# A second layer's input projections as seven products of halves instead of eight

## The chip, the cores and the metric

One core of a Trainium2 chip. The number is the device time of one execution in microseconds (us). The kernel before was run three times: 1753.05, 1754.44 and 1762.82 us, a median of 1754.44. One further execution was recorded by the profiler; every row below is of that one.

## What is computed

An encoder of two residual layers on 512 tokens of width 2048, in float32. Layer 0 mixes a gated DeltaNet and grouped query attention, and ends in an output projection with a residual. Layer 1, which the change is about, is a gated MLP:

```python
def gmlp_layer(x, norm_g, w_in, ln_g, ln_b, w_s, b_s, w_out):
    h = rms_norm(x, norm_g)
    u, v, gate = jnp.split(h @ w_in, 3, axis=-1)
    u = jax.nn.gelu(u, approximate=False)
    v = layer_norm(jax.nn.gelu(v, approximate=False), ln_g, ln_b)
    vc = v.reshape(bsz, n, C_CHUNK, C_GROUPS, cg)
    s = jnp.einsum('gts,bnsgc->bntgc', w_s, vc) + jnp.transpose(b_s)[None, None, :, :, None]
    z = u * s.reshape(bsz, L, C_WIDTH) * jax.nn.silu(gate)
    return x + z @ w_out
```

`h @ w_in` is 512 x 2048 by 2048 x 6144: one third each for u, v and gate.

## The kernel before

All big products are made by `proj` (L245) in groups of 512 output columns, in this order: layer 0's input groups, O0 to O3 (layer 0's output projection), VV0 to VV3 (v of layer 1), GG0, UU0, GG1, UU1 up to UU3 (gate and u in turn), R0 to R3 (layer 1's output projection). A group is 16 K-blocks of 128 rows of the weights. For one K-block each of the four blocks of 128 tokens takes three matmuls of 128x512 into its own PSUM bank, because every float32 operand is held as a high part (fp32r) and a rest: high by high, high by rest, rest by high (L276 to L278). That is 12 matmuls per K-block, 192 per group.

`load_raw` (L214) brings the weights, two K-blocks in one 512 KB transfer on SyncE's queue, into three buffers `raw`. `split` (L223) makes the high part `whi` by a cast on ScalarE (L231) and the rest `wlo` by a subtraction on VectorE (L232). `proj` calls it for the K-block at hand and the next two, and there are three buffers of each, so a split can begin when the K-block three back has been used. Splits run over the group's end into the next group.

When a group's last K-block is issued, the group is evacuated from its four banks: `evac` of O (L1252, L1255: residual and squares), of VV (L1294, Gelu, then BN_STATS2 at L1299), of GG (L1332, Silu), of UU (L1339, Gelu). All other work is written as generators in three lanes; `sub` (L171), called between the blocks of matmuls, runs as much of them as a rate allows, so an engine's order is that of the calls. `force` drains a lane for a result that is needed at once. The background work of this part: `h1_turn` (h = normalised x, transposed and split), `layer_norm1` (L1305, over v, which stays in SBUF), `spatial` (L1342: for each of 16 groups of 128 columns the product with w_s, times u and gate, and transposes to z), and `z_split` (L1403), whose first two row blocks are made ten K-blocks into UU3. Every engine works its instructions off in order.

## Time and profile before

| | |
|---|---|
| median of three runs | 1754.44 us (1753.05 to 1762.82) |
| span of the profiled execution | 1752.8 us (of its own whole time nothing more is recorded) |
| TensorE busy | 1723.6 us, 98% of the span |
| VectorE, ScalarE, GpSimd busy | 870.7, 718.6, 214.5 us |
| memory read and written | 125 GB/s over the span |

The span runs from the first to the last instruction of the one recorded execution. Busy time counts an engine's computing instructions; matmuls overlap in the array, so TensorE's busy share says that it always had work, not how fast it did it. Chain shares are of the span, along the chain of instructions and waits that ended last.

### The profile page before, as it was taken

How to read it: one execution, taken by the hardware profiler on the slowest of the kernel's cores; microseconds unless marked ns; L12 is line 12 of the kernel's file. 1: busy time of each engine (PE TensorE's matmuls, PEld its weight loads, DVE VectorE, ACT ScalarE, POOL GpSimd, SP SyncE). 2: the span in 40 equal slices, each digit the busy share in tenths (PEclk: the TensorE clock that was granted, in tenths of full speed). 3: DMA queues.
4: the chain of work that ended last, by engine and by line, in shares of the span. 5: the costliest groups of instructions: out<-in, count | busy, mean ns of one | idle time of the engine just before them, and what ended most of it. 6: DMA issues, size and time to landing. Idle time of an engine off the chain costs nothing.

```text
span 1752.8 us, 22461 instructions
## 1 busy us (share of the span) xinstructions
PE 1723.6 (98%) x8285; PEld 1426.1 (81%) x8285; DVE 870.7 (50%) x1544; ACT 718.6 (41%) x1463; POOL 214.5 (12%) x247
## 2 busy tenths in 40 slices
PE   8999998999999999999999999999999999999999
PEld 8888886787888998888788888888888888888887
DVE  4555599642764777876533333337342424235332
ACT  6444443524655555665422332222343433343221
POOL 0110055420200323540100000000000000000000
PEclk9999999979999999999999999999999999999999
DMA  5534642695464556434534443332323233333443
GB/s 191 140 94 123 127 115 81 138 200 146 116 172 122 165 162 193 148 94 157 169 121 137 144 156 97 96 97 89 105 89 96 84 96 90 96 109 100 145 140 109
DMA packets 212797, 221.30 MB, mean 126 GB/s; under 512 B 97857, under 2 KB 124785, under 8 KB 212688
## 3 DMA queue, kind: packets, MB, share of 16 engines
q1 hardware_dynamic: 211104, 215.33, 42.3%
q0 software_dynamic: 1408, 4.40, 1.0%
q8 instruction: 65, 1.06, 0.3%
q14 instruction: 44, 0.36, 0.1%
q10 hardware_dynamic: 176, 0.14, 0.0%
HBM read 186.18 MB, written 33.65 MB: 125 GB/s over the span
## 4 chain that ended last, share of the span: by engine, by line
PE 88%; DVE 5%; ACT 2%; issue 2%; SPq 1%; DMA 1%; POOL 0%; ACTq 0%; DVEq 0%; POOLq 0%
PE acc L277 20%; PE acc L276 20%; PE acc L278 20%; PE acc L272 5%; PE acc L273 5%; PE acc L274 5%; PE su L864 1%; DVE wlo L232 1%; PE mg L755 1%; PE aux L84 1%; DVE cv L437 1%; DMA raw<-in_w_in_dram 1%; PE sc L846 1%; PE po L1095 1%; DVE pr L661 1%
## 5 line engine op out<-in xcount | busy, mean ns | idle before, releaser
L232 DVE TENSOR_TENSOR wlo<-raw,whi 128x512 fp32r<-128x512 f32 (+1 forms) x544 | 387.8, 714 | 733.0 <-ACT whi L231 725.6
L231 ACT CAST whi<-raw 128x512 fp32r<-128x512 f32 (+1 forms) x544 | 330.0, 607 | 721.1 <-PE acc L278 534.5
L276 PE MATMUL acc<-whi,h1h 128*128 128x512 f32 x768 | 304.5, 396 | 0.0
L278 PE MATMUL acc<-whi,h1l 128*128 128x512 f32 x768 | 303.3, 395 | 0.0
L277 PE MATMUL acc<-wlo,h1h 128*128 128x512 f32 x768 | 303.3, 395 | 0.0
L272 PE MATMUL acc<-hTh,whi 128*128 128x512 f32 x512 | 211.9, 414 | 0.9 <-ACT whi L231 0.9
L274 PE MATMUL acc<-hTh,wlo 128*128 128x512 f32 x512 | 204.3, 399 | 7.2 <-DVE wlo L232 7.2
L273 PE MATMUL acc<-hTl,whi 128*128 128x512 f32 x512 | 203.5, 398 | 0.0
L278 PEld LDWEIGHTS acc<-whi,h1l 128*128 128x128 f32 x768 | 144.0, 187 | 35.1
L277 PEld LDWEIGHTS acc<-wlo,h1h 128*128 128x128 f32 x768 | 144.0, 188 | 34.8
L276 PEld LDWEIGHTS acc<-whi,h1h 128*128 128x128 f32 x768 | 144.0, 187 | 34.5
L276 PE MATMUL acc<-whi,hTh 128*128 128x352 f32 (+1 forms) x384 | 161.6, 421 | 1.4 <-ACT whi L231 1.4
L277 PE MATMUL acc<-wlo,hTh 128*128 128x352 f32 (+1 forms) x384 | 139.9, 364 | 3.1 <-DVE wlo L232 3.1
L278 PE MATMUL acc<-whi,hTl 128*128 128x352 f32 (+1 forms) x384 | 139.2, 363 | 0.0
L274 PEld LDWEIGHTS acc<-hTh,wlo 128*128 128x128 f32 x512 | 96.8, 189 | 32.9 <-DVE wlo L232 9.8
L272 PEld LDWEIGHTS acc<-hTh,whi 128*128 128x128 f32 x512 | 97.0, 189 | 19.4 <-ACT whi L231 1.0
L273 PEld LDWEIGHTS acc<-hTl,whi 128*128 128x128 f32 x512 | 97.1, 190 | 18.5
L276 PE MATMUL acc<-whi,zh 128*128 128x512 f32 x224 | 87.2, 389 | 0.0
L277 PE MATMUL acc<-wlo,zh 128*128 128x512 f32 x224 | 86.9, 388 | 0.0
L278 PE MATMUL acc<-whi,zl 128*128 128x512 f32 x224 | 86.9, 388 | 0.0
L277 PEld LDWEIGHTS acc<-wlo,hTh 128*128 128x128 f32 x384 | 74.1, 193 | 10.0 <-DVE wlo L232 4.5
L278 PEld LDWEIGHTS acc<-whi,hTl 128*128 128x128 f32 x384 | 73.4, 191 | 8.6
(315 smaller groups left out, 2489.9 us busy)
## 6 DMA issues: line engine op xcount, KB each, us to landing
raw<-in_w_in_dram SPq DMA_DIRECT2D x184, 512.0 KB, 3.8
raw<-in_w_out_dram SPq DMA_DIRECT2D x64, 512.0 KB, 3.7
raw<-in_w_in_dram SPq DMA_DIRECT2D x24, 352.0 KB, 4.1
...
```

The lines of the kernel that those rows point to most:

```text
L84: nc.tensor.transpose(out=o, in_=i, identity=ident[:k, :k])
L231: nc.scalar.copy(hi[:, :n], raw[:, a, :n])
L232: nc.vector.tensor_sub(lo[:, :n], raw[:, a, :n], hi[:, :n].bitcast(F32))
L272: mm(pt, lhsT=hi[:, s], rhs=ah, start=f, stop=False)
L273: mm(pt, lhsT=hi[:, s], rhs=al, start=False, stop=False)
L274: mm(pt, lhsT=lo[:, s], rhs=ah, start=False, stop=l)
L276: mm(pt, lhsT=ah[:, s], rhs=hi[:, cs], start=f, stop=False)
L277: mm(pt, lhsT=ah[:, s], rhs=lo[:, cs], start=False, stop=False)
L278: mm(pt, lhsT=al[:, s], rhs=hi[:, cs], start=False, stop=l)
L437: nc.vector.scalar_tensor_tensor(v[:, a:b], s[:, a + o:b + o], tp(j), v[:, a:b], ALU.mult, ALU.add)
L661: eng.tensor_tensor(pr, M[:, z, j + 1:, j:j + 1].to_broadcast(sj), W[:, z, j:j + 1, 0:n].to_broadcast(sj), op=ALU.mult)
L755: mm(pt[:, gs], lhsT=bd[:, w, g, :], rhs=src[:, gs], start=True, stop=True)
```

## The change

VV, GG and UU are made by a new function `fast` instead of `proj`. It halves tokens, K and the group's columns: 256 tokens by 256 columns, with each K-slab of 512 rows holding four quarters B11, B12, B21, B22 of the weights. Instead of eight products of quarters it makes seven (one level of Strassen's scheme in Winograd's form), each a sum over four slabs: of B11, B21, B22 and of four differences of quarters, T1 to T4. Each product has its own PSUM bank for the whole group.

- A unit is one product in one slab: 28 units per group, each 12 matmuls of 128x256. A product's first matmul (`opening`) is 128x512, with a half of zeros, and so starts the whole bank. The look-ahead of two units and the three buffers stay; `whi` is now three places in one constant tile.
- `tee` makes T1 to T4 of a slab on GpSimd, 16 subtractions of 128x512 per group (in `ex`); `split` works on quarters and differences, 28 times a group.
- `operands` makes the seven combinations of h that the products take: per pair of K-blocks four sums on GpSimd, three casts and three subtractions. Those of the second half of K follow O3, within VV0. For them O's evacuation keeps a scaled copy `xs` (one more activation per tile).
- `combine` puts the products together: one copy and seven additions per group. A product's turn comes in the unit behind its last one; T4's comes behind the group. Activations follow in place on T1's and T4's turn, two each, and for v the stores and BN_STATS2.
- v goes to DRAM (`v_d`) and comes back in tiles of 128 columns, which `spatial` normalises one by one. z goes to DRAM too, as far as it is ready before R0, and z's first two row blocks are split between UU3 and R0 (`z_firsts`). w_s is loaded on SyncE's queue, the layer norm's gains by each `spatial`. R's residual tiles are loaded later in their group.

```diff
+    FAST = {f"{m}{j}" for m in ("VV", "GG", "UU") for j in range(4)}
+    ORDER = ("B11", "B21", "B22", "T2", "T1", "T3", "T4")
+    units, start_of = [], {}
+    for gi, g in enumerate(groups):
+        start_of[g[0]] = len(units)
+        units += [(gi, k) for k in range(28 if g[0] in FAST else KT)]
     LOOK = 2
...
+        if nm in FAST:
+            src = w[(q // 2) * 512:(q // 2 + 1) * 512, c0:c0 + n].rearrange("(a e p) c -> e p a c", p=P, e=2)[q % 2]
...
+    whi_ = cst("whi", [P, 2 * LOOK + 3, 256], F32R)
+    nc.scalar.activation(whi_[:, 2 * LOOK + 2, :], ones.unsqueeze(1).to_broadcast([P, 2, P]), AF.Copy, scale=0.0)
+    def whi(u):
+        r = 2 * (u % (LOOK + 1))
+        return whi_[:, r:r + 2, :].rearrange("p a c -> p (a c)")
+    def opening(u):
+        r = 2 * (u % (LOOK + 1))
+        return whi_[:, r::2 * LOOK + 2 - r, :][:, 0:2, :]
...
+    def tee(gi, sl, nm):
+        t = ex(int(nm[1]) - 1).rearrange("p (a c) -> p a c", a=2)
+        q = lambda z: quarter(gi, sl, z)
+        a, b = {"T1": (lambda: (q("B12"), q("B11"))), "T2": (lambda: (q("B22"), tees[gi, sl, "T1"])),
+                "T3": (lambda: (q("B22"), q("B12"))), "T4": (lambda: (q("B21"), tees[gi, sl, "T2"]))}[nm]()
+        nc.gpsimd.tensor_tensor(t, a, b, op=ALU.subtract)
+        tees[gi, sl, nm] = t
+    def ahead(u):
+        for d, nm in ((2, "T1"), (1, "T2"), (0, "T3"), (-1, "T4")):
+            if 0 <= u + d < len(units):
+                gi, k = units[u + d]
+                if groups[gi][0] in FAST and k % 7 == (0 if d >= 0 else 1 + d) and (gi, k // 7, nm) not in tees:
+                    tee(gi, k // 7, nm)
+                    if nm in ("T3", "T4"):
+                        gone[0] = gi * 8 + (k // 7) * 2 + (1 if nm == "T3" else 2)
...
-        raw = raws[qi]
-        hi = sb.tile([P, 512], F32R, tag="whi", bufs=LOOK + 1, name=uid("whi"))
+        gi, k = units[u]
+        nm, _, _, n, _ = groups[gi]
+        hi = whi(u)
         lo = sb.tile([P, 512], F32R, tag="wlo", bufs=LOOK + 1, name=uid("wlo"))
-        nc.scalar.copy(hi[:, :n], raw[:, a, :n])
-        nc.vector.tensor_sub(lo[:, :n], raw[:, a, :n], hi[:, :n].bitcast(F32))
-        splits[i] = (hi, lo)
-        if a == 0:
-            load_raw(qi + 2)
+        if nm in FAST:
+            sl, o = k // 7, ORDER[k % 7]
+            src = quarter(gi, sl, o) if o[0] == "B" else tees[gi, sl, o]
+            v = lambda z: z.rearrange("p (a c) -> p a c", a=2)
+        else:
+            qi, a = gi * 8 + k // 2, k % 2
+            src = raws[qi][:, a, :n]
+            v = lambda z: z[:, :n]
+            if a:
+                gone[0] = qi + 1
+        nc.scalar.copy(v(hi), src)
+        nc.vector.tensor_sub(v(lo), src, v(hi).bitcast(F32))
+        splits[u] = (hi, lo)
...
+    def fast(name, ops, evac, late=None, func=None, rate=0.2):
+        u0 = pos[0]
+        gi = units[u0][0]
+        assert groups[gi][0] == name and u0 == start_of[name], name
+        bank = {o: (chain() if z in (4, 5) else aux("prod") if z == 6 else acc()) for z, o in enumerate(ORDER)}
+        todo = []
+        for u in range(u0, u0 + 28):
+            sl, o = (u - u0) // 7, ORDER[(u - u0) % 7]
+            pump()
+            for z in range(LOOK + 1):
+                split(u + z)
+            ahead(u)
+            if late is not None and u == u0 + 21:
+                late()
+            if func is not None and u == u0 + 20:
+                warm(func)
+            hi, lo = splits[u]
+            for kk in range(2):
+                a = ops(sl * 2 + kk)
+                for tb in range(2):
+                    out = bank[o][:, tb * 256:tb * 256 + 256]
+                    ah, al = (a(o, w)[:, tb * P:(tb + 1) * P] for w in range(2))
+                    h, l = (z[:, kk * 256:kk * 256 + 256] for z in (hi, lo))
+                    e = sl == 3 and kk == 1 and tb == 1
+                    if sl == 0 and kk == 0 and tb == 0:
+                        mm(bank[o], lhsT=ah, rhs=opening(u), start=True, stop=False)
+                    else:
+                        mm(out, lhsT=ah, rhs=h, start=False, stop=False)
+                    mm(out, lhsT=ah, rhs=l, start=False, stop=False)
+                    mm(out, lhsT=al, rhs=h, start=False, stop=e)
+                if kk == 0 and todo:
+                    evac(*todo.pop(0))
+                sub(1.0, rate)
+            splits.pop(u)
+            if sl == 3:
+                todo.append((o, bank))
+        for z in todo:
+            evac(*z)
+        pos[0] = u0 + 28
+    def combine(dst):
+        t = {}
+        def f(o, bank):
+            v = lambda z: bank[z].rearrange("p (t c) -> p t c", t=2)
+            tt = lambda a, b, c: nc.vector.tensor_add(a, b, c)
+            if o == "B11":
+                t["1"] = st("pp", [P, 2, 256])
+                nc.scalar.copy(t["1"], v(o))
+            elif o == "B21":
+                tt(dst("C11"), v(o), t["1"])
+            elif o == "T2":
+                t["2"] = st("pp", [P, 2, 256])
+                tt(t["2"], v(o), t["1"])
+                tt(dst("C12"), v("B22"), t["2"])
+            elif o == "T1":
+                tt(dst("C12"), v(o), dst("C12"))
+            elif o == "T3":
+                tt(t["2"], v(o), t["2"])
+                tt(dst("C22"), v("T1"), t["2"])
+            elif o == "T4":
+                tt(dst("C21"), v(o), t["2"])
+        return f
...
             spill(x1_d[t * P:(t + 1) * P, js], z)
+            xs.append(st("xs", [P, 512]))
+            nc.scalar.activation(xs[t], z, AF.Copy, scale=sc1[:, t:t + 1])
             jk = st("jk", [P, 512])
-            nc.scalar.activation(jk, z, AF.Square, accum_out=ss1[:, t, j:j + 1])
+            nc.scalar.activation(jk, xs[t], AF.Square, accum_out=ss1[:, t, j:j + 1])
...
+        g = lambda x, y, z, op: nc.gpsimd.tensor_tensor(x, y, z, op=op)
+        g(s[:, 0], a21, a22, ALU.add)
+        g(s[:, 1], s[:, 0], a11, ALU.subtract)
+        g(s[:, 2], a11, a21, ALU.subtract)
+        g(s[:, 3], a12, s[:, 1], ALU.subtract)
+        for src, z in ((hq[:, :, 0:256], opA[b][:, i]), (a22, opH[0][:, p])):
+            nc.scalar.copy(z[:, 0], src)
+            nc.vector.tensor_sub(z[:, 1], src, z[:, 0].bitcast(F32))
+            yield 0.8
+        yield -3
+        z = opS[p // 2][:, p % 2]
+        nc.scalar.copy(z[:, 0], s)
+        nc.vector.tensor_sub(z[:, 1], s, z[:, 0].bitcast(F32))
+        yield 1.2
...
+        def f(o, bank):
+            gu(o, bank)
+            if o in ("T1", "T4"):
+                for t in ((0, 1) if o == "T1" else (2, 3)):
+                    z = into[t // 2][:, t % 2, :]
+                    front.add(stats(z, t, j))
+                    spill(v_d[j * 4:j * 4 + 4, :, t, :].rearrange("g p c -> p g c"), z.rearrange("p (g c) -> p g c", g=4))
...
+    def fast_gu(into, func):
+        into.extend(m4("gu", [P, 2, 512]) for _ in range(2))
+        dst = lambda c: into[c[1] == "2"][:, :, (c[2] == "2") * 256:(c[2] == "2") * 256 + 256]
+        com = combine(dst)
+        def f(o, bank):
+            com(o, bank)
+            if o in ("T1", "T4"):
+                for t in range(2):
+                    z = into[o == "T4"][:, t, :]
+                    tt = t + 2 * (o == "T4")
+                    nc.scalar.activation(z, z, func, scale=rs1[:, tt:tt + 1])
+        return f
...
-        proj(f"VV{j}", act1, evac_v1(j), func=AF.Gelu if j == 0 else None)
...
+        fast(f"VV{j}", act1, fast_v1(j), func=AF.Gelu if j == 0 else None, rate=0.3)
...
+    def z_firsts():
+        for k in range(2):
+            z_split(k, zld.pop(k))
...
-        proj(f"GG{j}", act1, gate_evac(sgs), func=AF.Silu)
-        proj(f"UU{j}", act1, u_evac(us), func=AF.Gelu, late=(lambda: (z_split(0), z_split(1))) if j == 3 else None)
+        fast(f"GG{j}", act1, fast_gu(sgs, AF.Silu), func=AF.Silu)
+        fast(f"UU{j}", act1, fast_gu(us, AF.Gelu), func=AF.Gelu, late=z_first if j == 3 else None)
         front.add(spatial(j, us, sgs))
-    # ---------------- final projection ----------------
+    z_firsts()
```

The change moves work at the ends of the groups. Three places show it; the numbers behind tile names tell buffers apart.

VectorE where GG0 ends and UU0 begins, before: the subtractions of `split` (`wlo`) of UU0's first four K-blocks, with one row of `layer_norm1`.

```order
L232 TENSOR_TENSOR wlo_10607<-raw_10530,whi_10606 128x512
L1322 TENSOR_TENSOR vt_9446<-vt_9446,lg_10335 128x1024
L232 TENSOR_TENSOR wlo_10626<-raw_10530,whi_10625 128x512
L232 TENSOR_TENSOR wlo_10652<-raw_10571,whi_10651 128x512
L232 TENSOR_TENSOR wlo_10670<-raw_10571,whi_10669 128x512
```

The same place with the change: `acc`, `chain` and `prod` are PSUM banks, `gu` the group's result, `pp` a running sum.

```order
L308 TENSOR_TENSOR wlo_11849<-ex_8882,whi 128x512
L427 TENSOR_TENSOR pp_11858<-acc_11436,pp_11808 128x512
L427 TENSOR_TENSOR gu_11431<-acc_11435,pp_11858 128x2x256
L308 TENSOR_TENSOR wlo_11867<-raw_11700,whi 128x512
L427 TENSOR_TENSOR gu_11431<-chain_11437,gu_11431 128x2x256
L308 TENSOR_TENSOR wlo_11886<-raw_11796,whi 128x512
L427 TENSOR_TENSOR pp_11858<-chain_11438,pp_11858 128x512
L427 TENSOR_TENSOR gu_11432<-chain_11437,pp_11858 128x2x256
L427 TENSOR_TENSOR gu_11432<-prod_11439,pp_11858 128x2x256
L308 TENSOR_TENSOR wlo_11916<-raw_11796,whi 128x512
```

The first row is unit 27, the last of GG0; the three other subtractions are UU0's units 0, 1 and 2. Six additions that were not there lie between them: two for T2, T1's ahead of unit 1, and T3's two and T4's ahead of unit 2.

ScalarE at the same place, before: four activations of GG0's results stand between the casts of UU0's K-blocks 1 and 2, in one piece.

```order
L231 CAST whi_10606<-raw_10530 128x512
L231 CAST whi_10625<-raw_10530 128x512
L1332 ACTIVATE sg_1828_10632<-acc_10316,rs_9140 128x512
L1332 ACTIVATE sg_1828_10632<-acc_10317,rs_9140 128x512
L1332 ACTIVATE sg_1829_10641<-acc_10318,rs_9140 128x512
L1332 ACTIVATE sg_1829_10641<-acc_10319,rs_9140 128x512
L231 CAST whi_10651<-raw_10571 128x512
L231 CAST whi_10669<-raw_10571 128x512
```

And with the change:

```order
L430 COPY pp_11808<-acc_11433 128x512
L307 CAST whi<-ex_8882 128x512 x3
L307 CAST whi<-raw_11700 128x512
L1527 ACTIVATE gu_11431<-gu_11431,rs_8933 128x512 x2
L307 CAST whi<-raw_11796 128x512
L1527 ACTIVATE gu_11432<-gu_11432,rs_8933 128x512 x2
L307 CAST whi<-raw_11796 128x512
L307 CAST whi<-ex_8882 128x512 x4
```

The three casts from `raw` are those of UU0's units 0, 1 and 2. T1's two activations, which take what VectorE's additions leave, now stand ahead of unit 1's cast, and T4's two ahead of unit 2's.

ScalarE where UU3 ends and R0 begins, with the change (`z` and `zl` are z's row blocks, from DRAM):

```order
L307 CAST whi<-raw_14868 128x512
L1527 ACTIVATE gu_14573<-gu_14573,rs_8933 128x512 x2
L307 CAST whi<-raw_14868 128x512
L1527 ACTIVATE gu_14574<-gu_14574,rs_8933 128x512 x2
L1554 CAST z_1974_15101<-zl_14969 128x512
L1554 CAST z_1975_15102<-zl_14971 128x512
L307 CAST whi<-raw_14985 128x512
```

The casts of z's first two row blocks, which R0's first matmuls take, have come from the middle of UU3 to behind T4's activations.

## Rows read from the trace of the kernel before

**Rows 1.** The page: the span, and the shares of the chain that ended last

```profile
span 1752.8 us, 22461 instructions
...
PE 88%; DVE 5%; ACT 2%; issue 2%; SPq 1%; DMA 1%; POOL 0%; ACTq 0%; DVEq 0%; POOLq 0%
```

**Rows 2.** Windows view, O0's end to UU3's end: busy us (instructions) per engine

```profile
core 0: us, PE busy (x) PEld busy (x) DVE busy (x) ACT busy (x) POOL busy (x), PEclk, DMA share, GB/s
870.00:1602.00 732.00, 732.00 (x3216) 589.61 (x3215) 276.32 (x427) 250.30 (x434) 8.82 (x13) 1.00 0.35 107
```

**Rows 3.** Timeline within VV3: start us, us, engine, line, operation [idle before <-releaser]

```profile
1200.44 0.39 PE L278 MATMUL acc<-whi,h1l 128*128 128x512 f32 x1
...
1200.67 0.40 PE L276 MATMUL acc<-whi,h1h 128*128 128x512 f32 x1
...
1200.87 0.62 ACT L231 CAST whi<-raw 128x512 fp32r<-128x512 f32 x1 [2.18 <-PE acc L278]
...
1203.67 0.62 ACT L231 CAST whi<-raw 128x512 fp32r<-128x512 f32 x1 [2.18 <-DVE vt L1322]
...
1204.32 0.69 DVE L232 TENSOR_TENSOR wlo<-raw,whi 128x512 fp32r<-128x512 f32 x1 [0.66 <-ACT whi L231]
```

**Rows 4.** Timeline of PE at R3's end: first and last of 18 such

```profile
1747.12 0.28 PE L276 MATMUL acc<-whi,zh 128*128 128x256 f32 x1
...
1749.10 0.28 PE L278 MATMUL chain<-whi,zl 128*128 128x256 f32 x1
```

**Rows 5.** Timeline where GG0 ends, ScalarE and then VectorE

```profile
1234.47 0.62 ACT L231 CAST whi<-raw 128x512 fp32r<-128x512 f32 x1 [2.18 <-PE acc L278]
1235.17 2.79 ACT L1332 ACTIVATE sg<-acc,rs 128x512 f32<-128x512 f32 x4
1237.86 0.61 ACT L231 CAST whi<-raw 128x512 fp32r<-128x512 f32 x1
...
1238.50 0.69 DVE L232 TENSOR_TENSOR wlo<-raw,whi 128x512 fp32r<-128x512 f32 x1 [2.68 <-ACT whi L231]
```

**Rows 6.** Groups by line and shape; the first three within 1055 to 1560 us

```profile
L232 DVE TENSOR_TENSOR wlo<-raw,whi 128x512 fp32r<-128x512 f32 x175 | 121.0, 692 | 299.6 <-ACT whi L231 299.2
L231 ACT CAST whi<-raw 128x512 fp32r<-128x512 f32 x175 | 108.5, 620 | 311.6 <-PE acc L278 307.3 <-DVE vt L1320 2.2 <-DVE vt L1322 2.2
L1299 DVE BATCH_NORM_STATS2 bst<-vt 128x6 f32<-128x512 f32 x16 | 11.1, 694 | 0.4
...
L426 ACT ACTIVATE cv<-cs,taps 128x512 f32<-128x512 f32 x24 | 17.3, 719 | 4.6 <-DVE cs L505 2.7 <-POOL cs L503 1.8
L1252 DVE TENSOR_TENSOR xr<-acc,xr 128x512 f32<-128x512 f32 x16 | 9.9, 683 | 0.0
L1255 ACT ACTIVATE jk<-xr 128x512 f32<-128x512 f32 x16 | 9.9, 620 | 5.4 <-DVE xr L1252 5.4
L1148 ACT ACTIVATE sgb<-sgb 128x512 f32<-128x512 f32 x8 | 5.0, 630 | 0.0
L1255 ACT ACTIVATION_READ_ACCUMULATOR jk<-xr 128x1 f32 x16 | 3.0, 186 | 0.0
```

**Rows 7.** Timeline of DVE and of POOL in O0, two meetings of the two

```profile
836.37 1.36 DVE L232 TENSOR_TENSOR wlo<-raw,whi 128x512 fp32r<-128x512 f32 x1 [0.60 <-ACT whi L231]
...
847.81 1.37 DVE L232 TENSOR_TENSOR wlo<-raw,whi 128x512 fp32r<-128x512 f32 x1 [1.21 <-ACT whi L231]
...
835.90 1.29 POOL L1153 TENSOR_TENSOR ybTl<-yo,ybTh 128x512 fp32r<-128x512 f32 x1 [40.96 <-ACT ybTh L1150]
...
847.33 1.30 POOL L1153 TENSOR_TENSOR ybTl<-yo,ybTh 128x512 fp32r<-128x512 f32 x1 [3.86 <-ACT ybTh L1150]
```

**Rows 8.** Windows view, columns as in rows 2: two stretches in which TensorE waited

```profile
262.00:275.00 13.00, 7.59 (x33) 5.25 (x31) 12.69 (x17) 3.47 (x6) 11.74 (x17) 1.00 0.14 40
...
350.00:353.00 3.00, 1.04 (x5) 0.86 (x5) 2.97 (x3) 0.65 (x2) 2.92 (x2) 1.00 0.98 312
353.00:357.00 4.00, 4.00 (x12) 3.08 (x11) 3.77 (x4) 1.69 (x3) 1.90 (x2) 0.57 0.99 173
...
373.00:391.00 18.00, 17.61 (x70) 15.93 (x70) 5.82 (x6) 3.29 (x6) 0.95 (x1) 0.53 1.00 228
```

More of the change, by code (lines that the diff above doesn't have):

```diff
@@ new lines, in ahead, with split @@
+    def ahead(u):
[6 more added lines that the diff above has]
+                        gone[0] = gi * 8 + (k // 7) * 2 + (1 if nm == "T3" else 2)
+    def split(u):
+        if u >= len(units) or u in splits:
@@ L1276, in encoder @@
     for j in range(4):
         out0_group(j)
+    done.add("O3")
     rs1 = cst("rs1", [P, NT])
@@ L1342, in spatial, with layer_norm1 @@
-    def spatial(j, us, sgs):
-        ws = st("ws", [P, 4, P])
-        nc.gpsimd.dma_start(ws, c_ws1[0, j * 4:(j + 1) * 4].rearrange("g t s -> t g s"))
+    def layer_norm1():
+        while v_ready[0] < 16:
+            yield -1
+        for t in range(NT):
+            nc.vector.bn_aggr(mv[:, 0:2, t], bst[:, t].rearrange("p a b -> p (a b)"))
+        nc.vector.tensor_scalar(mv[:, 2, :], mv[:, 1, :], EPS, None, ALU.add)
+        rsqrt(mv[:, 3, :], mv[:, 2, :])
+        done.add("ln")
+        yield 1.0
@@ new lines, in encoder, with z_home @@
+    for j in range(4):
+        fast(f"VV{j}", act1, fast_v1(j), func=AF.Gelu if j == 0 else None, rate=0.3)
+    stored("v1")
+    front.add(layer_norm1())
+    z_h, z_l, zs = [], [], {}
+    def z_home(k):
+        if k in zs:
+            return zs[k]
+        if k < 2:
+            if 0 not in zs:
+                z = [m4("z01", [P, 2, T], F32R) for _ in range(2)]
+                zs[0], zs[1] = ((y[:, 0, :], y[:, 1, :]) for y in z)
+        else:
+            i, j = divmod(k - 2, 8)
+            while len(z_h) <= i:
+                z_h.append(big("zh", [P, 8, T], F32R))
+                z_l.append(big("zl", [P, 8, T], F32R))
+            zs[k] = z_h[i][:, j, :], z_l[i][:, j, :]
+        return zs[k]
@@ new lines, in z_split, with v_load, v_norm, v_split @@
+    def z_split(k, src):
+        hi, lo = z_home(k)
+        nc.scalar.copy(hi, src)
+        nc.vector.tensor_sub(lo, src, hi.bitcast(F32))
+        done.add(("zs", k))
+    def spatial(j, us, sgs):
+        yield from until("v1", "ln")
+        g4 = lambda z: z.rearrange("p (a t) -> p a t", a=4)
+        lg = [st("lg", [P, 512]) for _ in range(2)]
+        for z, src in zip(lg, (c_ln_g1, c_ln_b1)):
+            nc.gpsimd.dma_start(z, src[0:1, j * 512:(j + 1) * 512].to_broadcast([P, 512]))
+        ws = g4(ex(4))
+        nc.sync.dma_start(ws, c_ws1[0, j * 4:(j + 1) * 4].rearrange("g t s -> t g s"))
+        def v_load(a):
+            z = g4(ex(5 + a % 2))
+            nc.sync.dma_start(z, v_d[j * 4 + a])
+            return z
+        def v_norm(a):
+            for n in range(NT):
+                nc.vector.tensor_scalar(vr[:, n, :], vr[:, n, :], mv[:, 0, n:n + 1], mv[:, 3, n:n + 1],
+                                        ALU.subtract, ALU.mult)
+            for z, op in zip(lg, (ALU.mult, ALU.add)):
+                nc.vector.tensor_tensor(vr, vr, z[:, a * P:(a + 1) * P].unsqueeze(1).to_broadcast([P, NT, P]), op=op)
+        def v_split():
+            vh, vl = st("vh", [P, 512], F32R), st("vl", [P, 512], F32R)
+            nc.scalar.copy(g4(vh), vr)
+            nc.vector.tensor_sub(g4(vl), vr, g4(vh).bitcast(F32))
+            return vh, vl
+        vr = v_load(0)
@@ L1439, in out_group, with load @@
         js = slice(j * 512, (j + 1) * 512)
-        xr = [st("xo", [P, 512]) for _ in range(NT)]
-        for t in range(NT):
-            nc.sync.dma_start(xr[t], x1_d[t * P:(t + 1) * P, js])
+        xr = []
+        def load():
+            for t in range(NT):
+                xr.append(st("xo", [P, 512]))
+                nc.sync.dma_start(xr[t], x1_d[t * P:(t + 1) * P, js])
         def evac(t, pt):
```

262 lines of the change are left out of this document (138 added, 124 removed).

## Prediction

> **What bounds the kernel now.** I began with the windows view of the stretch from the output projection to the end of the input projections: TensorE is busy for 732.00 of 732.00 us at a granted clock of 1.00 (the upper level, 2.4 GHz), VectorE for 276, ScalarE for 250, GpSimd for 9 [rows 2]. The chain that ended last is TensorE for 88% of the span [rows 1]. So here matmul columns are time, and the other engines have room as long as nothing makes TensorE wait for them. Two price lists follow from the timeline. A 128x512 matmul starts 0.23 us after the one before [rows 3]; the eighteen 128x256 matmuls at the end of the program start from 1747.12 to 1749.10, that is 1.98 us for 17 steps, 0.1165 each, every one with its own weight load [rows 4]. And the split that feeds TensorE: the ScalarE cast starts 0.04 us after the last matmul of the K-block whose buffer it takes over has ended (1200.44 + 0.39 to 1200.87), lasts 0.62, and VectorE's subtraction starts 0.03 later and lasts 0.69 [rows 3].
>
> How much room there is at a group's end shows where GG0 ends: four activations of together 2.79 us stand between two casts, and the next cast starts at 1237.86, the subtraction after it at 1238.50 [rows 5]; yet TensorE loses nothing [rows 2], because a K-block lasts 12 x 0.233 = 2.80 us and the split runs two K-blocks ahead. After the change a unit lasts 12 x 0.1165 = 1.40 us, with the same split to make and the same look-ahead of two.
>
> **The change, part by part.**
>
> *TensorE.* Twelve groups had 16 x 12 = 192 matmuls of 512 columns: 2304 x 0.2333 = 537.6 us. Now they have 28 x 12 = 336 of 256 columns, of which 7 (the openings) are 512 wide: 4032 x 0.1165 + 84 x 0.1165 = 479.5 us. That is **-58 us**.
>
> *Steady units.* Cast and subtraction of unit u+2 end about 0.24 + 0.62 + 0.03 + 0.69 = 1.6 us after unit u starts, and are needed at 2.9. That holds with 1.3 us to spare, so I cost the 12 more splits of a group at nothing between the ends.
>
> *A group's end.* The order shows what the room must hold. VectorE used to do only subtractions there; now seven combining additions lie among them, and ScalarE's activations come in two pairs, each behind an addition, with casts behind each pair. Durations: an addition that reads PSUM 0.683, a subtraction 0.692, an activation from SBUF 0.630, a cast 0.620 [rows 6]. I put 0 where the next group's unit 0 would begin. The subtraction of unit 27 can end at -2.6. Behind it VectorE does two additions (-1.25), unit 0's subtraction (-0.55) and T1's addition (+0.1). The two activations wait for that (1.4), unit 1's cast is behind them (2.0), its subtraction ends at 2.7: unit 1, due at 1.5, is **1.2 us late**. Then come three additions, the last with T4's product (4.8), two activations (6.0), unit 2's cast (6.65) and subtraction (7.35). Unit 2 could begin at 2.7 + 1.4 = 4.1 and begins some 3.1 later. So **4.3 us of waiting per group end**, however early the products were ready: it is the order on two engines that sets it. In the v groups two BN_STATS2 of 0.694 [rows 6] stand in this chain, of which one lies on the path: 5.0. Where the previous spatial gate's normalisation of v stands between T1's addition and unit 1's subtraction (three of the GG to UU ends) I add 0.5. Sum: four ends after VV groups 20.0, GG to UU 4.3 + 3 x 4.8 = 18.7, UU to GG 3 x 4.3 = 12.9: **+52 us**.
>
> *O3 to VV0.* The O groups' evacuation has one more activation per tile: 0.72 for the scaled copy [rows 6], so that with square and accumulator read a tile takes 0.72 + 0.62 + 0.19 = 1.5 us of ScalarE, four of them 6.1 where it was 3.2, ahead of VV0's third cast. Between 0 (all hidden) and 6, I take **+3**.
>
> *UU3 to R0.* The casts of z's first two row blocks stand behind T4's two activations, and R0's first matmuls need them: 6.0 + 0.62 + 0.03 + 0.69 = 7.3 for the first block. Before, they were done ten K-blocks into UU3. **+7**.
>
> *The end of R0.* K-blocks 14 and 15 take z from the last spatial gate, whose turning now stands right before them in TensorE's order. Product, evacuation, transposes, cast and subtraction one after the other make about 4 us, of which one and a half are covered for block 14: **+4.5** (0 to 8).
>
> *Normalisation of v inside groups.* Nine tiles lie inside groups, each six VectorE instructions in a row that hold up one subtraction. Margin 1.3 us, so I take 0.4 each: **+3.5** (0 to 10).
>
> *Work hidden at no cost.* 16 stores and 16 loads of v of 256 KB, 12 and 12 of z, the reloaded gains: DMA is busy at 0.35 [rows 2], and the loads are issued a tile ahead.
>
> *GpSimd.* It was idle here. Now it makes 16 weight differences of 128x512 per group and VV0's operands. Such an operation takes 1.29 to 1.30 us, and a VectorE subtraction that begins while one runs ends 0.54 us after it: the one begun at 836.37 beside the operation of 835.90 + 1.29 took 1.36, the next such one 1.37 [rows 7], against 0.692 [rows 6]. So a collision costs up to 0.67 us, about 0.33 on average; two subtractions of each group end can meet one, 22 x 0.33 = 7, and VV0, which has the operands on top (about 54 us of such work for a span of 48), 5 more: **+12** (0 to 30). The Trainium skill, "SBUF — State Buffer", section "SBUF: two separate sides", calls this an exclusive lock between GpSimd and a VectorE operation with two SBUF inputs, with the loser fully blocked. By it a delayed subtraction would run its whole 0.69 after the other's end; the rows show 0.54, so by the rule the term would be some 3 us larger.
>
> Sum: -58 + 52 + 3 + 7 + 4.5 + 3.5 + 12 = **+24 us**. The traced execution's span is 1752.8 us, 1.6 below the median of 1754.4; I set the sum on the median: **1778 us**.
>
> **Rivals.**
>
> *The ends are absorbed (faster).* If VectorE and ScalarE come through a group's end about 4 us sooner than I chain them, only the first 0.5 us of each end shows: -58 + 6 + 18 + 7 = -27, about 1727. For it: before, 2.79 us of activations in front of a cast cost nothing [rows 5]. Against it: that slack was two units of 2.80, now it is two of 1.40, and the casts stand behind waiting activations in a queue kept in order. It decides if unit 2's cast starts before about +1.6 after the old group's end instead of 6. Chance 0.12.
>
> *The ends cost what the products save (same).* The chain holds, but the five small terms and the collisions stay at their lower ends: -58 + 52 + 7 = about +1, 1755. Chance 0.20.
>
> *The clock falls at the ends (slower still).* After a stretch in which TensorE was busy for 1.04 of 3.00 us the granted clock was 0.57 over the next 4 us, and 0.53 in 373 to 391, the lower level, 1.2 GHz; but in 262 to 275, busy for 7.59 of 13.00, it stayed at 1.00 [rows 8]. So gaps of 1 and 3 us may or may not do it. A fall like the first takes about 4 x 0.43 = 1.7 us, eleven of them 19: 1797; one like the second takes 8.5. The Trainium skill, "TensorE: Matmul & The Clock Gate", section "HAM oscillation", tells of kernels in which each wait drops the clock anew; the trace has both outcomes. Chance 0.13.
>
> *GpSimd and VectorE together are full (slower still).* Per group 16 x 1.29 + 28 x 0.692 = 40.0 us against 336 x 0.1165 + 0.8 = 40.0 us of TensorE. If they can't overlap at all, a pair of gate groups, with its two products of 128x1024 and the tiles of v on top, takes some 9 us more than TensorE's own time; the waits at two ends cover just that, or, where they don't fall together, up to 5 a pair remain: about 1798. Chance 0.05.
>
> **How the numbers follow.** Forecast 0.50, the rivals 0.12, 0.20, 0.13 and 0.05. The forecast's own range is 1763 to 1800: small terms low without most of the collisions, or high. For eight in ten I go from 1750, which leaves out the faster rival, to 1818, the clock rival with a few long falls. No change means within 0.5%, 8.8 us, about what a measurement of this kernel can tell, so 1745.7 to 1763.2. Faster 0.12; same 0.20; slower 0.68, which is the forecast and the last two rivals.
>
> **What would show it.** In the changed profile: 128x256 matmuls 0.117 apart inside groups and groups of about 40 us of TensorE work; at each group's end two waits of TensorE for a subtraction, about 1 and 3 us, on unit 1 and unit 2; VectorE's additions back to back there; ScalarE idle before T1's activations, waiting for VectorE; R0's first matmul about 7 us late; subtractions of 1.1 to 1.4 us where GpSimd is busy; the clock at 1.00. The forecast is wrong if the waits at the ends are under 2 us together, if units inside a group wait, if 128x256 matmuls need more than 0.12 us in the long run, or if the clock falls.

## The result, and the profile after

The changed kernel takes 1837.35 us (median of four runs, 1835.88 to 1848.47) against 1757.74 for the kernel before in the same series: 1.0468 times as long, with a 95% interval of 1.0429 to 1.0507. It is slower, as forecast, but by 80 us and not 24, and it lies above the range.

From the page of the changed kernel: the span, the engines' busy time, and the shares of the chain that ended last.

```profile
span 1835.2 us, 27028 instructions
...
PE 1719.4 (94%) x10013; PEld 1501.4 (82%) x10013; DVE 1177.5 (64%) x1836; ACT 831.2 (45%) x1641; POOL 542.2 (30%) x469
...
PE 71%; DVE 16%; issue 5%; ACT 5%; DMA 2%; POOL 1%; SPq 0%; ACTq 0%; DVEq 0%; POOLq 0%
```

TensorE's share of the chain has gone from 88% [rows 1] to 71%; VectorE and ScalarE now hold 21%. The windows view from VV0 to R0 answers to [rows 2]:

```profile
core 0: us, PE busy (x) PEld busy (x) DVE busy (x) ACT busy (x) POOL busy (x), PEclk, DMA share, GB/s
...
1020.00:1642.00 622.00, 544.79 (x4146) 517.17 (x4144) 493.85 (x575) 283.00 (x471) 317.12 (x216) 0.96 0.35 107
```

TensorE is no longer busy throughout, GpSimd works for half the time, and the clock is at 0.96 of its upper level. From VV0's first matmul to R0's first it was 1011.33 to 1565.50, 554.2 us; now it is 1020.11 to 1642.04, 621.9. Split by stage, by the first matmul of each, the two profiles differ like this:

| stage | before | after | difference |
|---|---|---|---|
| up to O0's start | 817.9 | 821.1 | +3.2 |
| O0 to O3 | 193.4 | 199.0 | +5.6 |
| VV0 to UU3 | 554.2 | 621.9 | +67.8 |
| R0 to the end | 187.3 | 193.2 | +5.9 |
| span | 1752.8 | 1835.2 | +82.4 |

Where VV2 ends and VV3 begins, the timeline of ScalarE, then VectorE, GpSimd and TensorE (waits alone):

```profile
1176.65 1.33 ACT L1527 ACTIVATE gu<-gu,rs 128x512 f32<-128x512 f32 x2 [3.72 <-DVE gu L427]
1177.90 0.60 ACT L307 CAST whi<-raw 128x512 fp32r<-128x512 f32 x1
1181.77 1.33 ACT L1527 ACTIVATE gu<-gu,rs 128x512 f32<-128x512 f32 x2 [3.28 <-DVE gu L427]
1183.01 0.60 ACT L307 CAST whi<-raw 128x512 fp32r<-128x512 f32 x1
...
1171.60 1.46 DVE L308 TENSOR_TENSOR wlo<-ex,whi 128x512 fp32r<-128x512 f32 x1 [0.24 <-ACT whi L307]
1172.99 0.68 DVE L427 TENSOR_TENSOR pp<-acc,pp 128x512 f32<-128x512 f32 x1
1173.70 0.69 DVE L427 TENSOR_TENSOR gu<-acc,pp 128x512 f32<-128x512 f32 x1
1174.31 1.71 DVE L308 TENSOR_TENSOR wlo<-raw,whi 128x512 fp32r<-128x512 f32 x1
1175.94 0.68 DVE L427 TENSOR_TENSOR gu<-chain,gu 128x512 f32<-128x512 f32 x1
...
1178.53 0.69 DVE L308 TENSOR_TENSOR wlo<-raw,whi 128x512 fp32r<-128x512 f32 x1 [0.42 <-ACT whi L307]
...
1181.07 0.67 DVE L427 TENSOR_TENSOR gu<-prod,pp 128x512 f32<-128x512 f32 x1
1183.65 0.69 DVE L308 TENSOR_TENSOR wlo<-raw,whi 128x512 fp32r<-128x512 f32 x1 [1.91 <-ACT whi L307]
...
1170.90 1.62 POOL L277 TENSOR_TENSOR ex<-raw,ex 128x512 f32<-128x512 f32 x1
1172.48 1.75 POOL L277 TENSOR_TENSOR ex<-raw,raw 128x512 f32<-128x512 f32 x1
1174.18 1.29 POOL L277 TENSOR_TENSOR ex<-raw,ex 128x512 f32<-128x512 f32 x1
...
1176.07 0.39 PE L409 MATMUL acc<-wlo,opA 128*128 128x256 f32 x1 [0.76 <-DVE wlo L308]
...
1178.55 0.51 PE L406 MATMUL acc<-whi,opA 128*128 128x512 f32 x1 [0.92 <-ACT whi L307]
...
1183.67 0.79 PE L406 MATMUL acc<-whi,opS 128*128 128x512 f32 x1 [2.84 <-ACT whi L307]
```

Read it from the top: ScalarE idles 3.72 us for VectorE's addition before it may do T1's activations, with unit 1's cast behind them; then 3.28 us for T4's addition, with unit 2's cast behind those. TensorE waits for these two casts, 0.92 and 2.84 us. While ScalarE waits, VectorE is busy without a break, and two of its subtractions last 1.46 and 1.71 us instead of 0.69. Each began beside a GpSimd operation and ended 0.54 to 0.55 us after it (1172.52 and 1175.47). The additions, which read a PSUM bank, take their usual 0.68 and 0.69 us beside GpSimd. The matmul after the long wait takes 0.79 us, where the same form took 0.40 and 0.51 before it: the clock has fallen. The windows view shows it:

```profile
1184.00:1188.00 4.00, 4.00 (x17) 3.51 (x17) 2.89 (x6) 1.28 (x3) 1.19 (x1) 0.50 0.75 224
```

Three waits away from these ends, where the forecast has a term for the first and the last: TensorE's first in VV0, the one ahead of h's transposes behind O0, and R0's first matmul:

```profile
1025.65 0.50 PE L406 MATMUL acc<-whi,opS 128*128 128x512 f32 x1 [2.32 <-ACT whi L307]
...
879.14 0.33 PE L84 MATMUL aux<-ident,xs 128*128 128x128 f32 x1 [1.04 <-ACT xs L1405]
...
1642.04 0.79 PE L351 MATMUL acc<-whi,z 128*128 128x512 f32 x1 [6.63 <-ACT z L1554]
```

Taken from the starts of successive matmuls, less the usual 0.117 us, the twelve groups wait for 99 us. Matmuls at the lower level add 22: 1.4 to 2.9 us at nearly every end. The product work is smaller by 58, as computed.

### The profile page after: what moved, and what is told of

Same layout as the page of the kernel before. It is cut to its first block, busy times and chain, and to the rows that moved or that the text cites. A ratio compares the mean times of both kernels' runs of the same rounds, so it can differ in the third digit from the quotient of the medians.

```text
span 1835.2 us, 27028 instructions
## 1 busy us (share of the span) xinstructions
PE 1719.4 (94%) x10013; PEld 1501.4 (82%) x10013; DVE 1177.5 (64%) x1836; ACT 831.2 (45%) x1641; POOL 542.2 (30%) x469
## 4 chain that ended last, share of the span: by engine, by line
PE 71%; DVE 16%; issue 5%; ACT 5%; DMA 2%; POOL 1%; SPq 0%; ACTq 0%; DVEq 0%; POOLq 0%
PE acc L352 9%; PE acc L353 9%; PE acc L351 9%; DVE wlo L308 6%; PE acc L347 5%; PE acc L348 5%; PE acc L349 5%; PE acc L409 4%; PE acc L410 3%; PE acc L408 3%; ACT whi L307 2%; DVE ex L1574 1%; PE chain L409 1%; DVE gu L427 1%; PE chain L410 1%
## 5 line engine op out<-in xcount | busy, mean ns | idle before, releaser
L308 DVE TENSOR_TENSOR wlo<-ex,whi 128x512 fp32r<-128x512 f32 x192 | 180.7, 956 | 69.3 <-ACT whi L307 68.3
L307 ACT CAST whi<-ex 128x512 fp32r<-128x512 f32 x192 | 118.2, 621 | 152.5 <-PE acc L410 136.1
L277 POOL TENSOR_TENSOR ex<-raw 128x512 f32<-128x512 f32 x48 | 68.1, 1419 | 312.4 <-DVE wlo L308 244.1
L277 POOL TENSOR_TENSOR ex<-raw,ex 128x512 f32<-128x512 f32 x96 | 150.8, 1571 | 13.3 <-DMA raw<-in_w_in_dram 5.8
L409 PE MATMUL acc<-wlo,opA 128*128 128x256 f32 x384 | 111.3, 290 | 11.8 <-DVE wlo L308 11.7
L409 PE MATMUL acc<-wlo,opS 128*128 128x256 f32 x384 | 117.2, 305 | 5.2 <-DVE wlo L308 5.1
L409 PE MATMUL chain<-wlo,opS 128*128 128x256 f32 x384 | 108.3, 282 | 11.5 <-DVE wlo L308 11.4
L410 PE MATMUL acc<-whi,opS 128*128 128x256 f32 x384 | 114.8, 299 | 0.2 <-DVE opS L1456 0.2
L410 PE MATMUL acc<-whi,opA 128*128 128x256 f32 x384 | 107.9, 281 | 1.2 <-DVE opA L1451 1.2
L410 PE MATMUL chain<-whi,opS 128*128 128x256 f32 x384 | 107.0, 279 | 0.0
L408 PE MATMUL acc<-whi,opS 128*128 128x256 f32 x360 | 107.0, 297 | 0.0
```

Source lines behind the costliest of these rows:

```text
L277: nc.gpsimd.tensor_tensor(t, a, b, op=ALU.subtract)
L307: nc.scalar.copy(v(hi), src)
L308: nc.vector.tensor_sub(v(lo), src, v(hi).bitcast(F32))
L408: mm(out, lhsT=ah, rhs=h, start=False, stop=False)
L409: mm(out, lhsT=ah, rhs=l, start=False, stop=False)
L410: mm(out, lhsT=al, rhs=h, start=False, stop=e)
```

## The experiments

Twelve kernels ran, each with a profile; ten of them ran once, the late evacuation twice and the last version twelve times. A time is the median of a kernel's runs, the other columns are of the one profiled execution. The stage up to O0 is the same in all of them, but its length differed by up to 10 us with how long the clock stayed at its lower level near 375 us (13.7 to 41 us), so I compare the section from VV0 to R0, which lies behind that stage. Group lengths in us, from first matmul to first matmul:

| kernel | time | VV0 | VV2 | UU0 | GG2 | UU2 | VV0 to UU3 | R |
|---|---|---|---|---|---|---|---|---|
| before | 1754.4 | 46.5 | 44.8 | 44.8 | 49.7 | 44.8 | 554.2 | 187.3 |
| changed | 1837.4 | 58.2 | 48.0 | 47.8 | 53.2 | 51.9 | 621.9 | 193.2 |
| late evacuation | 1801.0 | 58.2 | 43.2 | 42.1 | 53.3 | 49.5 | 584.8 | 191.5 |
| no differences | 1803.5 | 50.0 | 47.1 | 45.6 | 49.1 | 49.1 | 581.0 | 193.7 |
| fill, mended | 1821.4 | 58.3 | 46.8 | 46.3 | 53.1 | 50.3 | 608.5 | 192.9 |
| z and transposes | 1842.4 | 58.3 | 48.4 | 47.6 | 53.6 | 52.5 | 616.4 | 198.0 |
| v on ScalarE | 1799.3 | 58.2 | 43.2 | 42.1 | 47.1 | 50.9 | 571.1 | 197.8 |
| all of these | 1798.7 | 58.2 | 43.2 | 42.0 | 53.4 | 47.3 | 577.8 | 197.0 |
| rest at the ends | 1784.7 | 58.3 | 43.2 | 42.1 | 51.7 | 44.6 | 564.2 | 197.1 |
| half on VectorE | 1763.4 | 58.6 | 41.8 | 42.3 | 47.1 | 46.3 | 551.4 | 196.2 |
| R0's rate | 1757.2 | 57.1 | 42.0 | 42.3 | 47.2 | 46.2 | 550.0 | 191.7 |
| VV on VectorE | 1758.5 | 53.9 | 42.5 | 42.4 | 47.2 | 46.2 | 548.5 | 191.8 |
| last version | 1751.7 | 47.5 | 42.2 | 40.9 | 47.8 | 44.3 | 538.0 | 191.6 |

**Late evacuation.** `combine` and the activations hand back closures with a delay in units; `fast` and `proj` run one unit's worth behind the split.

```diff
-                if kk == 0 and todo:
-                    evac(*todo.pop(0))
+                if kk == 0:
+                    step()
...
+                "T3": [(0, lambda: tt(t["2"], v(o), t["2"])), (1, lambda: tt(dst("C22"), v("T1"), t["2"]))],
+                "T4": [(0, lambda: tt(dst("C21"), v(o), t["2"]))]}[o]
...
+                    out.append((1, act))
```

> Edit: at a group's end the additions and activations are issued one or two units later, behind the splits of the next group's units, so that no cast stands behind an activation that waits; nothing else differs. Theory O (the order on ScalarE and VectorE makes the waits): the waits of a plain group end fall from 6.3 us (VV2 in the changed kernel) to under 2, the clock stays at 1.00 at most ends, a VV group lasts 41 to 43 us instead of 48, and the time falls by 55 to 80 us to 1757 to 1782. Theory P (the subtractions are late because GpSimd's differences block them): the waits stay at 5 us or more, the time falls by less than 20 us. Theory C (the clock falls whatever the waits): low periods at every end remain, and some 20 us of the gain stay away.

The ratio to the kernel before fell from 1.0468 to 1.0236 (1.0160 to 1.0312). VV2's wait fell from 6.3 to 2.5 us, where under 2 was expected, VV1 to UU0 show no low clock at all, and a VV group, at 43.2 us, is now shorter than before the change. VectorE at the same end:

```profile
1168.27 1.19 DVE L308 TENSOR_TENSOR wlo<-raw,whi 128x512 fp32r<-128x512 f32 x1
...
1170.77 0.68 DVE L308 TENSOR_TENSOR wlo<-raw,whi 128x512 fp32r<-128x512 f32 x1
...
1172.77 0.69 DVE L308 TENSOR_TENSOR wlo<-raw,whi 128x512 fp32r<-128x512 f32 x1
```

The subtractions of units 0, 1 and 2 now start 2.5 and 2.0 us apart; in the changed kernel (1174.31, 1178.53, 1183.65) they were 4.2 and 5.1 apart. So theory O holds for the ends up to UU0, and theory C falls: the low clock goes with the waits. The time fell by 36 us, 37 of them in this section, instead of 55 to 80: VV0 kept its 58.2, and GG1 to UU3 still wait, in part in new places inside the groups.

**No differences.** `tee` computes nothing; the splits of T1 to T4 read a constant tile.

> Edit: the 16 GpSimd weight differences of every group are left out; the splits of T1 to T4 read a constant tile instead, so the output isn't the reference's. Theory O: about 1.2 us of the 6.3 at an end, VV0's collisions and the waits inside GG groups go, the rest stays: 20 to 35 us less, 1802 to 1817, an end still waits 4.5 to 5 us, and the clock still falls there. Theory P: an end's waits fall under 2 us and the time falls by 60 us or more.

Section: 41 us less; the time fell by 34, as the stage up to O0 was 7 longer. The ends still wait 4.5 us after VV groups and 4.1 in UU0, which is the chain of the forecast without collisions (5.0 and 4.3 there), and the clock still falls at each. VV0 wins 8 us, not by the end of collisions alone: in the changed kernel two of its casts wait for a difference itself, which stands behind the operands in GpSimd's order, 3.86 us here and 3.68 at the second. In VV1 to UU3 no cast waits for GpSimd.

```profile
1033.66 0.62 ACT L307 CAST whi<-ex 128x512 fp32r<-128x512 f32 x1 [3.86 <-POOL ex L277]
```

Theory O, then, with collisions that cost about three times what I had put (41 us against 12). The subtractions show it, grouped by line within 1078 to 1580 us; first the changed kernel:

```profile
L308 DVE TENSOR_TENSOR wlo<-ex,whi 128x512 fp32r<-128x512 f32 x160 | 149.4, 947 | 57.1 <-ACT whi L307 56.1
L308 DVE TENSOR_TENSOR wlo<-raw,whi 128x512 fp32r<-128x512 f32 x120 | 142.3, 1204 | 38.1 <-ACT whi L307 37.7
L1574 DVE TENSOR_SCALAR ex<-ex,mv 128x128 f32<-128x128 f32 x40 | 21.5, 597 | 0.0
...
L277 POOL TENSOR_TENSOR ex<-raw,ex 128x512 f32<-128x512 f32 x80 | 126.1, 1576 | 6.0 <-DVE wlo L308 2.8
```

and the kernel without differences:

```profile
L308 DVE TENSOR_TENSOR wlo<-ex,whi 128x512 fp32r<-128x512 f32 x168 | 114.3, 690 | 87.8 <-ACT whi L307 86.3
L308 DVE TENSOR_TENSOR wlo<-raw,whi 128x512 fp32r<-128x512 f32 x127 | 87.8, 692 | 99.5 <-ACT whi L307 99.1
...
L1574 DVE TENSOR_SCALAR ex<-ex,mv 128x128 f32<-128x128 f32 x48 | 13.3, 342 | 0.0
```

A subtraction takes 0.69 us alone and 0.95 to 1.20 on average beside the differences, which themselves take 1.58 instead of the 1.30 of [rows 7].

**Fill.** Matmuls ahead of units 1 and 2, so that TensorE works while it would wait. The first try:

```diff
+            if u - u0 in FILL and name != "VV0":
+                for _ in range(FILL[u - u0]):
+                    mm(bank["T4"], lhsT=filler[0], rhs=filler[1], start=True, stop=True)
+            filler[:] = [ops(0)(o, 0)[:, 0:P], hi]
```

> Edit: in every group but VV0, 4 matmuls of 128x512 ahead of unit 1 and 10 ahead of unit 2 (0.9 and 2.3 us), into the bank that T4's first matmul starts afresh, so that TensorE works while it would wait. If the waits make the clock fall: no low periods at the ends of VV1 to UU3, the waits of 128x256 matmuls there shrink by what is filled, and the time falls by 12 to 20 us to 1817 to 1825 although work is added. If the clock falls for another reason (the 256-column matmuls themselves, say): the low periods stay, and the time stays or rises by up to 10 us.

It took 1908 us and can't decide: the filling matmuls read the `whi` buffer that the cast of three units on had just been issued into, and so waited for that cast; VV1 to UU3 got 5 to 7 us longer each. Mended, with operands that are there and T2's bank:

```diff
+                    mm(bank["T2"][:, 0:256], lhsT=ops(0)("B11", 1)[:, 0:P], rhs=ops(0)("B11", 0), start=True, stop=True)
```

> Edit, in the changed kernel: the fill of the run before, mended. In every group but VV0, 8 matmuls of 128x256 ahead of unit 1 and 20 ahead of unit 2 (0.9 and 2.3 us), into the bank of T2, which has been read by then, from operands of h that are long there, so that they wait for nothing. If the waits make the clock fall: no or few low periods at the ends of VV1 to UU3, and 12 to 20 us less than the changed kernel's 1837 although TensorE has 36 us more to do. If it falls for another reason: the low periods stay and the time doesn't fall.

1821 us: 16 less, of which 13.4 in the section, with 36 us of matmuls added. Windows view, 1078 to 1583 us, of the changed kernel and of this one:

```profile
1078.00:1583.00 505.00, 449.01 (x3441) 427.05 (x3441) 403.41 (x470) 222.67 (x366) 252.50 (x169) 0.97 0.35 108
```

```profile
1078.00:1583.00 505.00, 480.24 (x3807) 457.77 (x3808) 415.06 (x486) 229.10 (x377) 259.78 (x170) 1.00 0.36 110
```

With the waits filled the clock stays at 1.00, and the 22 us of slow matmuls in the section are down to 2. So the waits made it fall, and some 20 us is the price of it, separately from the waits.

**z and transposes.** z's first row blocks are split in UU3, and h's transposes come later.

```diff
-            if late is not None and u == u0 + 21:
-                late()
+            if late is not None and u - u0 in (17, 20, 22):
+                late(u - u0)
...
-        yield -2
+        yield -2 if j == 3 else -4
...
-    z_firsts()
```

> Edit: (1) z's first two row blocks are loaded at unit 17 and split at units 20 and 22 of UU3 instead of between UU3 and R0; (2) the transposes of h after O0 to O2 are issued four slices after the group instead of two. Theory: (1) takes 6.6 us at R0's start down to the plain end's 5 or less, and its part of the low clock with it, 2 to 4 us less; (2) takes the three waits of 1.9 us each ahead of the transposes of O1 to O3 away, 5 to 6 us less. Together 1827 to 1831. Rival: the splits inside UU3 and the later transposes make waits of their own, and nothing is won.

A miss by the time, 1842 instead of 1827 to 1831, but 9 us of that lie in the stage up to O0, which the edit doesn't touch. In what it does touch the gain is 3.5 us instead of 6 to 10. UU3 lost its wait for z (52.1 us instead of 58.9), but R grew by 4.8: R0's wait moved on to the next row block, whose load was issued only at 1647, 4.52 us:

```profile
1652.93 0.79 PE L351 MATMUL acc<-whi,zh 128*128 128x512 f32 x1 [4.52 <-ACT zh L1554]
```

The transposes' part gave 2.8 of 5.6 us: O0 to O3 took 196.2.

**v on ScalarE, and what was put on top.** Four further steps, each on the kernel before it.

```diff
-                nc.vector.tensor_scalar(vr[:, n, :], vr[:, n, :], mv[:, 0, n:n + 1], mv[:, 3, n:n + 1], ALU.subtract, ALU.mult)
+                nc.scalar.activation(vr[:, n, :], vr[:, n, :], AF.Identity, scale=mv[:, 3, n:n + 1], bias=mb[:, n:n + 1])
```

> Edit, on top of the late evacuation: v's centring and scaling by four ScalarE activations per tile instead of four VectorE operations, the gain's and the bias's operations and the products by the gate issued one at a time. Theory O: the long waits inside GG1 to UU3 (1.5 to 3.1 us, one VectorE burst each) go, with the low clock behind them: a GG group from 53.3 to 46 to 48 us, a UU group from 49.5 to 46 to 47, 18 to 28 us less than 1801. Theory P (the subtractions are short of VectorE time as GpSimd blocks them): the waits only move, less than 8 us.

The section fell by 13.7 us, the low clock in GG1 to UU3 went, and GG2 is at 47.1, but UU2 rose to 50.9: half a confirmation. The time fell by under 2 us instead of 18 to 28, since the stage up to O0 was 4 longer and R grew by 6. For R I suspect the last gate's new pauses; the run with R0's rate shortens them, but raises that rate too.

```diff
-    def fast(name, ops, evac, late=None, func=None, rate=0.2):
+    def fast(name, ops, evac, late=None, func=None, rate=0.3):
...
+            if late is not None and u - u0 in (17, 22, 24):
+                late(u - u0)
...
+        yield -2 if j == 3 else -7
```

> Edit: the run before, with z's first four row blocks loaded at unit 17 of UU3 and the first two split at its units 22 and 24, with O0's to O2's transposes seven slices behind the group instead of two, and with a rate of 0.3 instead of 0.2 for the gate and u groups. Expected: R0 starts 2 to 4 us earlier after UU3, O0 to O3 take 3 to 5.6 us less, 1768 to 1780.

O0 to O3 fell from 199.1 to 193.7 and UU3 from 53.0 to 47.6, as expected, but the time stayed at 1798.7 instead of 1768 to 1780. The higher rate undid it: GG groups went back to 53.4 us. Of GG2's 9 us of waits some 2 stand at its end; most of the others are in its first half.

```diff
-                sub(1.0, rate)
+                sub(1.0, (0.4 if 2 <= u - u0 <= 23 else 0.0) if name[0] != "V" else rate)
```

> Edit: the run before, with the background lanes of the gate and u groups at rest in units 0, 1 and 24 to 27 and at a rate of 0.4 in between. Theory O: the ends after GG1 to GG3 lose their remaining waits, 3 to 8 us less than the run before. Rival: the denser background makes as many waits in the middle, no difference.

13.6 us less in the section, more than the 3 to 8 expected: UU2 fell from 47.3 to 44.6, GG2 only from 53.4 to 51.7. So where the background stands counts, but it is not all: at the rate of 0.2 GG2 was at 47.1, and what it waits for now is again mostly in its first half, as the rival had it in part.

```diff
-        nc.gpsimd.tensor_tensor(t, a, b, op=ALU.subtract)
+        eng = nc.vector if nm in ("T1", "T3") else nc.gpsimd
+        eng.tensor_tensor(t, a, b, op=ALU.subtract)
```

> Edit: the run before (pause), with the differences T1 and T3 made by VectorE (0.69 us each, nothing to block) and only T2 and T4 by GpSimd. Theory P (after the order is mended, GpSimd and VectorE operations with two SBUF inputs, which hold each other up, are the bound: 16 x 1.29 + 28 x 0.69 = 40.0 us per group of 40.0 us, more with the spatial work): the sum falls to 8 x 1.29 + 36 x 0.69 = 35.2, GG1 to GG3 go from 51.7 to 46 to 49, VV1 to VV3 from 43.2 to 41 to 42, VV0 from 58 to 51 to 54: 15 to 30 us less than 1785. Theory O alone: VectorE has more to do in its order, so the waits stay or grow, 0 to 15 us more.

The section fell by 12.8 us, a little under what theory P said (the time by 21, with some 8 of it from the stage up to O0): VV2 41.8, GG2 47.1; UU2 rose by 1.7 and VV0 stayed at 58.6, where 51 to 54 was expected. Giving VectorE more to do made the kernel faster. That agrees with theory P, that with the order mended the two engines' common work is the bound; but the edit also changes which engine's order the differences stand in, and no run parts the two.

**R0's rate, VV on VectorE, last version.**

```diff
+        rate = RATES.get(name, RATE) if gi < 14 else 0.9 if name == "R0" else 0.45
...
+        yield -4 if j < 3 else -1
...
+            yield -2 if j < 3 else -1
```

> Edit: the run before, with shorter pauses in the last spatial gate and R0's background rate 0.9 instead of 0.45. Expected: the waits of R0 for the last row blocks of z (1.0, 3.0 and 1.0 us, and the low clock behind them) shrink, R0 to R3 go from 197 to 190 to 193 us, the rest is the same.

R fell from 196.2 to 191.7, as expected.

```diff
+        eng = nc.vector if nm in ("T1", "T3") or groups[gi][0][0] == "V" else nc.gpsimd
```

> Edit: the run before, with all four differences on VectorE in the v groups. Theory P: no collision there at all but in VV0 (operands), VV1 to VV3 at 40.5 to 41.5 us. Theory O: VectorE has 28 + 16 subtractions of 0.69, 7 additions of 0.68 and 4 statistics of 0.69, 38 us of 40, in order; the ends wait again, 43 us or more.

Between the theories: VV2 0.5 us worse, VV0 3.2 better. Only VV0, where GpSimd also makes the operands, gains by it.

```diff
+        eng = nc.vector if nm in ("T1", "T3") or groups[gi][0] == "VV0" else nc.gpsimd
...
+                    "T1": [(1, lambda: tt(dst("C12"), v(o), dst("C12")))],
+                    "T3": [(1, lambda: tt(t["2"], v(o), t["2"])), (2, lambda: tt(dst("C22"), v("T1"), t["2"]))],
+                    "T4": [(2, lambda: tt(dst("C21"), v(o), t["2"]))]}[o]
...
+                    out.append((2 + (o == "T4"), act))
...
+                carry[t + 2].append(square)
```

> Edit: the run with R0's rate, with one VectorE addition per unit at the ends (T1's, T3's and T4's additions one or two units later still, activations behind them by one more unit, background at rest in units 0 to 3), VV0's differences all on VectorE, O3's squares issued within VV0, and R0 stepping twice per K-block. Theory O: what is left at the ends (1.7 us after VV groups, 2 after the others, one unit with two additions and a difference each) falls under 1 us, VV0 from 57 to 49 to 53 us: 8 to 16 us less than 1757, so 1741 to 1749, under the kernel before's 1753 to 1763. Theory P: the ends keep their waits as VectorE has no time left there, 1752 to 1758, the same as before.

1751.71 us (median of 12 runs) beside 1754.98 for the kernel before (17 runs): ratio 0.9964, interval 0.9947 to 0.9982, a gain of 0.4%. That is between theory O's 1741 to 1749 and theory P's 1752 to 1758, and as five things changed at once it doesn't say which of them won what. VV0 came to 47.5 and the UU groups to 1 us of waits, as theory O has it; the GG groups kept 4.4 us. The windows and waits views of it, VV0 to R0:

```profile
1014.00:1552.00 538.00, 518.90 (x4146) 498.70 (x4146) 448.20 (x635) 297.43 (x515) 153.24 (x106) 1.00 0.39 123
```

```profile
PE acc L418 <- DVE wlo L309: 15.5, 24, 2.6
PE chain L418 <- DVE wlo L309: 1.7, 4, 0.9
```

So 16 of the 58 us that seven products save are there, at the same product work as in the changed kernel. The profiled execution, 1745.35 us, is one of the two fastest of the twelve; where the other ten lose 5 to 10 us more isn't recorded.

## Why the prediction was wrong in size

- **Product work, right.** 310 of VV2's 336 matmuls start 0.12 us after the one before; the saving of 58 us is real.
- **The ends, right.** The chain through two in-order engines came out as worked: waits on units 1 and 2, ScalarE idle ahead of both pairs of activations, 4.1 to 4.5 us without collisions against 4.3 to 5.0. The late evacuation, which changes the order alone, takes most of it away.
- **UU3 to R0, right.** 7 us put, 6.63 waited. **O3 to VV0, right:** 3 put, 3.1 in VV0's first two waits.
- **Collisions, mis-sized.** The term said +12, from two meetings per end at 0.33 us each and 5 for VV0, with 30 as its upper end. Without the differences the section is 41 us shorter: 33 in VV1 to UU3, where nothing waits for a difference itself, and 8 in VV0, where two casts do. At the end shown both subtractions met GpSimd, for 0.77 and 1.02 us: more than the 0.67 that I had as the most. The rule that I read from [rows 7] holds: 134 subtractions of VV1 to UU3 began beside one GpSimd operation and took longer, and each ended 0.54 to 0.56 us after it. What failed is the price taken from it. Both meetings of [rows 7] began 0.47 us into the operation; a subtraction that begins with it loses up to 1.1 us, and an operation that was itself held up lasts 1.6 to 1.8 us instead of 1.3. On average such a subtraction lost 0.8 us, and I counted 22 of them, though not each of the 134 holds TensorE up.
- **The clock, put on a rival.** I gave 0.13 to its falling at the ends and 19 us as its price, and left it out of the sum. It fell at 10 of the 11 ends and cost 22 us by the slower matmuls; the fill, which kept it up, made the section 13.4 us shorter although matmuls were added. The step that failed is the reading of [rows 8]: I took the stretch from 262 to 275 us, without a fall, as evidence that such gaps may be harmless, and weighed it like the one with a fall. The Trainium skill, "TensorE: Matmul & The Clock Gate", section "HAM oscillation", tells of a kernel that waits for data at every K-tile and is throttled anew each time. Its waits are longer than these, but this trace agrees that returning waits lower the clock again and again, with 0.50 from 1184 to 1188 at one of ten such ends.
- **O0 to O3, left out.** I charged the longer evacuation to VV0 alone. After O0, O1 and O2 h's transposes stand in TensorE's order and wait for it too, which makes each of the next groups 1.9 us longer, 5.6 in all; with the transposes issued later this is gone (193.7 us).
- **Small terms.** Normalisation of v: 3.5 put. GG1 to GG3 wait 9.1 to 9.2 us against 5.7 to 6.7 in groups with a plain end, UU1 and UU2 1.4 more than UU0: some 13 us. That these are mostly bursts of VectorE work beside GpSimd fits the run with v on ScalarE, but part of it stands in the collisions' 41 us already. R0's end: 4.5 put, R is 5.9 longer, two waits of 1 us and the rest low clock at R0's start.

That [rows 8] showed no fall was luck of that one execution. The same stretch of layer 0 in the changed kernel's profile, where the kernels are alike, with one wait of 2.39 us:

```profile
262.00:275.00 13.00, 10.51 (x40) 7.91 (x39) 12.76 (x19) 3.02 (x5) 11.90 (x15) 0.87 0.20 64
```

In 8 of the 14 profiles the clock fell there, with waits of 2.2 to 2.4 us. So such a wait may or may not lower it, and a single trace can't show that it is harmless.

In VV0 to UU3 the forecast had +20 us and the profile shows +68: of the 48 between, 22 are clock and some 29 collisions, with small errors the other way. Two of the forecast's own signs of being wrong are there, the fallen clock and waits inside GG and UU groups. GpSimd and VectorE being full together, which I gave 0.05, may be the next bound once the order is mended: that the half on VectorE won agrees with it, but doesn't show it alone. What stays open is the layer 0 stage: why its low clock lasted 14 to 41 us in kernels that are alike there.
